# Feed-forward output of an encoder block: order of the loads, and the last normalisation on one engine

## The chip, the cores and the metric

The kernel runs on one core of one Trainium2 chip. The metric is device time in microseconds (us) of a whole execution, and versions are compared by the median of several runs. The engines are named as the profile names them: PE (TensorE) multiplies matrices, DVE (VectorE), ACT (ScalarE) and POOL (GpSimd) work on tiles element by element, SP (SyncE) here only issues DMA transfers. Each engine works through a queue of its own in order, and waits on semaphores for the others.

## The reference, cut to what matters

One layer of an encoder block on 1024 tokens of width 1024: a projection, dilated attention and a gated recurrence, then a feed-forward part (`D_FF` is 2816). The change lies in the last line, in the product with `w_ffn_out` and the layer norm behind it.

```python
def layer_norm(x, g, b):
    xf = x.astype(jnp.float32)
    mu = jnp.mean(xf, axis=-1, keepdims=True)
    xc = xf - mu
    var = jnp.mean(xc * xc, axis=-1, keepdims=True)
    y = xc * lax.rsqrt(var + LN_EPS) * g.astype(jnp.float32) + b.astype(jnp.float32)
    return y.astype(x.dtype)
...
    h = layer_norm(DEEPNORM_ALPHA * h + merged @ w_o[l], ln1_g[l], ln1_b[l])
    gate, up = jnp.split(h @ w_ffn_in[l], 2, axis=-1)
    h = layer_norm(DEEPNORM_ALPHA * h + (jax.nn.silu(gate) * up) @ w_ffn_out[l], ln2_g[l], ln2_b[l])
```

## The kernel before, in words

The whole kernel is one long program, built by a tile framework that tracks the dependencies of tiles, hands out buffers from pools (a tile waits until the last reader of the buffer's former tile is done) and orders each engine's instructions by a schedule of its own. Where the kernel fixes an order by hand, it does so with `ordered(key, ...)`: the loads of this stage are all made by `queued`, so they stay on SP in the order in which the program asks for them, and the splits and sums of this stage are `ordered` on DVE under the key `"sums"`.

Stage by stage there are the projection with attention and recurrence, the merge, `ffn_in` and at last `ffn_out`, which the change touches. `ffn_in` writes the gated activations and sums of them to DRAM, one tensor `gd[p]` for each of seven products.

`ffn_out` multiplies the activations (1024 tokens x 2816) with `w_ffn_out` (2816 x 1024) as a 2 x 2 block product with seven products instead of eight (Strassen's scheme in Winograd's form). Each product p has 512 tokens, 512 columns and a depth of 11 tiles of 128 (index f). The list `seq` holds the steps (p, f) of the products 1, 2, 6, 5, 3 and 7, 66 in all. The last product, 4, is done token block by token block in 12 `chunks` (three for each of the four blocks g of 128 tokens), so that its rows end one after another.

All values are float32. Each operand is split into a rounded part `hi` and a remainder `lo`, and `mm3` makes three matmuls: hi x hi, hi x lo, lo x hi. One step is 4 token blocks x 3 = 12 matmuls of 128x512. In the profile's names `gwsum` and `gwkeep` are hi and lo of the activations (three buffers each), `w_hi` and `w_lo` those of the weights (four). `hi` is cast by ACT (L212), `lo` is subtracted by DVE (L222). PE runs matmuls at L270, L271 and L272: L270 and L272 use `w_hi`, L271 uses `w_lo`.

`prep(i)` prepares step i, three steps ahead of the matmuls (`AHEAD = 3`). It calls `acts`, which takes care of the activation loads, then asks for weight tiles up to a count that grows with i, then splits the weights and makes the sums of weights that later products need (`extra`, L1767). Activations come in pairs (two f in one load of 512 KB, tile `a_raw`); three pairs are held, two in a pool with two buffers and one in another. Weights come in tiles of 256 KB: `11`, `21`, `12`, `22` are the blocks of the matrix, and the first six of block row 1 were loaded in whole rows (`w_rows`, L1683) by `ffn_in`. The loads of this stage are asked for in program order on SP, so a load that waits for its buffer holds back all loads behind it.

When a product is complete, `out` adds it from PSUM to the rows `Y[t]` (eight tiles of 128 tokens x 1024, L1791) and takes statistics (L1793). `finish(t)` makes the layer norm of a row tile: mean and variance (L206, L207), the power -1/2 by POOL (L208), and then one of two forms. Row tiles 6 and 7 take the mean out and multiply with g in one fused DVE operation (L1804), multiply with the power and add b in a second (L1807), each in two halves of 512 columns. Row tiles 0 to 5 take a longer way: a shift on DVE (L292), the normalisation on ACT (L293), the product with g on POOL (L1812), the sum with b on DVE (L1813). Rows 0 to 2 are finished in the middle of product 7 and early in the chunks; row 3 and rows 4 to 7 follow while the chunks run. `store` writes rows 0 to 5 to DRAM a few steps later, from SP (L1825).

Of the kernel before, what the change touches and what calls it, by code (L numbers as in the profile page):

```python
# [10 lines left out]
F32 = mybir.dt.float32  # L11
# [3 lines left out]
OP = mybir.AluOpType  # L15
# [7 lines left out]
HALF = 512  # L23
# [56 lines left out]
class Block:  # L80
# [1609 lines left out]
    def ffn_out(self):  # L1690
# [4 lines left out]
        nc, NP = self.nc, NF // 2  # L1695
        with ExitStack() as es:
            fob = es.enter_context(self.pool("fob"))
# [9 lines left out]
            Y = [fob.tile([128, D], F32, name=f"y{t}") for t in range(8)]  # L1707
            bn = [fob.tile([128, 2, 6], F32, name=f"st{t}") for t in range(8)]
            g2, b2 = (fob.tile([128, D], F32, name=n) for n in ("g2", "b2"))

            def load(z, f):
                i, k = int(z[0]) - 1, int(z[1]) - 1
                r = 128 * (2 * f + i)
                self.queued(W[z, f], self.wfo[r:r + 128, HALF * k:HALF * (k + 1)])

            seq = [(p, f) for p in (1, 2, 6, 5, 3, 7) for f in range(NP)]
            loads = [("11", f) for f in range(EARLY, NP)]
# [3 lines left out]
            pairs = [(p, f, n % 3) for n, (p, f) in enumerate(z for z in seq if z[1] % 2 == 0)]  # L1721
            loaded, raws, ready, last, t2s = 0, {}, {}, {}, {}
# [8 lines left out]

            def acts(p, f):

                while len(raws) < 3 and pairs:
                    q, k, m = pairs.pop(0)
                    n = min(2, NP - k)
                    raws[q, k] = (self.wraw, self.wraw, self.abp)[m].tile(
                        [128, 2, HALF], F32, name="a_raw", tag="wraw", bufs=(2, 2, 1)[m])
                    self.queued(raws[q, k][:, :n], self.gd[q][:, k:k + n])
                r = raws[p, f - f % 2]  # L1740
                if f % 2 or f + 1 == NP:
                    del raws[p, f - f % 2]
                return pair(r[:, f % 2])

            def pair(src):
                n = src.shape[1]
                hi, lo = (self.ws.tile([128, HALF], F32R, name=f"g{tag}", tag=tag, bufs=3)[:, :n]
                          for tag in ("wsum", "wkeep"))
                self.split(hi, lo, src, eng_lo="dve", key="sums")
                return hi, lo  # L1750

            def weights(src):
                hi, lo = (z.rearrange("p k c -> p (k c)") for z in self.granules())
                self.split(hi, lo, src, eng_lo="dve", key="sums")
                return hi, lo

            def extra(z, f):
                b = {k: W.get((k, f)) for k in ("11", "12", "21", "22")}
                if z == "last":
                    last[f] = place("11", f, F32R), place("12", f, F32R)  # L1760
                    self.split(*last[f], b["21"], eng_lo="dve", key="sums")
                    return
                if z == "t2":
                    t2s[f] = fob.tile([128, HALF], F32, name="t2", tag="t2", bufs=NP)
                out, x, y = {"t1": (b["11"], b["12"], b["11"]), "t2": (t2s.get(f), b["22"], b["11"]),
                             "t4": (b["21"], b["21"], t2s.get(f)), "t3": (b["12"], b["22"], b["12"])}[z]
                self.ordered("sums", nc.vector.tensor_sub(out, x, y))  # L1767

            def prep(i):
                nonlocal loaded  # L1770
                if i >= len(seq):
                    return
                p, f = seq[i]
                a = acts(p, f)
                while loaded < min(len(loads), 4 + 3 * i // 2):
                    load(*loads[loaded])
                    loaded += 1
                src = t2s[f] if p == 6 else W[{1: "11", 2: "21", 5: "11", 7: "12", 3: "22"}[p], f]
                ready[i] = a, weights(src)
                for z in todo.get(i, ()):  # L1780
                    extra(*z)
# [11 lines left out]
                    nc.vector.bn_stats(bn[g + 4 * i][:, k, :], y)  # L1793

            def finish(t):
                y, halves = Y[t], t > 5
                mv = self.tiny.tile([128, 4], F32, name="mv2", tag="bnmv", bufs=3)
                self.rstd(mv, bn[t])
                if halves:
                    for n in range(2):  # L1800
                        for k in range(2):
                            s = slice(HALF * k, HALF * (k + 1))
                            if n == 0:
                                nc.vector.scalar_tensor_tensor(y[:, s], y[:, s], mv[:, 0:1], g2[:, s],  # L1804
                                                               op0=OP.subtract, op1=OP.mult)
                            else:
                                nc.vector.scalar_tensor_tensor(y[:, s], y[:, s], mv[:, 2:3], b2[:, s],  # L1807
                                                               op0=OP.mult, op1=OP.add)
                                nc.sync.dma_start(self.out[128 * t:128 * (t + 1), s], y[:, s])
                else:  # L1810
                    self.normalise(fob, y, y, mv)
                    nc.gpsimd.tensor_mul(y, y, g2)  # L1812
                    nc.vector.tensor_add(y, y, b2)  # L1813

            stores = []

            def end(t, now):
                finish(t)
                if t < 6:
                    stores.append((now + 3, t))  # L1820
# [7 lines left out]
            for i in range(AHEAD):  # L1828
                prep(i)
            for i, (p, f) in enumerate(seq):  # L1830
                prep(i + AHEAD)
                store(i)
                (ahi, alo), (bhi, blo) = ready.pop(i)
                if p in (1, 6) and 4 <= f < 8:
                    t = f if p == 6 else f - 4
                    self.queued(Y[t], self.ahs_d[t])
                if p == 5 and f < 2:
                    t, v = (g2, b2)[f], self.ln["2"][f]
                    self.queued(t, bass.AP(tensor=v.tensor, offset=v.offset, ap=[[0, 128], [1, D]]))
                for g in range(4):  # L1840
                    if f == 0 and p == 2:
                        banks[g][1] = self.ps_sd()
                    c = slice(128 * g, 128 * (g + 1))
                    self.mm3(banks[g][p in (2, 5, 3)], ahi[:, c], alo[:, c], bhi, blo, p in (1, 2, 5) and f == 0,
                             f == NP - 1, skip_group_check=True)
                    if f == NP - 1:
                        out(p, g)
                if p == 7 and f in (4, 8):
                    end(f // 4 - 1, i)

            chunks = [(g, f) for g in range(4) for f in range(0, NP, 4)]
            halves, acts4 = {}, {}
# [70 lines left out]
```

## Time and profile before

| | |
|---|---|
| three runs | 2068.7, 2071.84, 2070.64 us, median 2070.64 |
| the profiled execution | 2068.59 us, of which the span from the first to the last instruction is 2066.8 |
| mean granted clock of PE | 0.994 |
| busy: PE, DVE, ACT, POOL | 2014.9, 1324.6, 953.3, 1078.9 us |
| product stage `ffn_out` | from about 1850 us to the end |

Times in the profile's rows are counted from the start of the span. A row of the timeline has start, duration, engine, line, operation, output and inputs, a count, and in brackets the idle time before it with what ended it. A row of waits has the waiting engine and line, the releaser, and total, count and longest. A row of a group has the count, then busy time and mean in ns, then idle time. A row of a stretch has from:to, its length, the busy time and count of PE, PE's weight loads, DVE, ACT and POOL, the granted clock, the DMA engines' busy share and GB/s. Operations of one engine overlap by about a tenth of a microsecond at their ends.

### The profile page before, as it was taken

What the parts mean: (1) busy time and instruction counts of PE and PEld (TensorE: products, weight loads), DVE (VectorE), ACT (ScalarE), POOL (GpSimd) and SP (SyncE); (2) the same over time, 40 slices, a digit from 0 to 9 for tenths busy, and PEclk for the clock granted to TensorE, in tenths of its full rate; (3) what the DMA queues carried; (4) which work ended last, traced back from release to release, by engine and by line L of the source; (5) the groups of instructions that cost most, each with busy time, mean ns of one, the idle gap of its engine ahead of it and who ended that gap; (6) DMA issues with size and microseconds to landing.
All of it is one profiled execution on the core that took longest, in us unless ns stands there. A gap on an engine that the chain in (4) does not pass through costs nothing. (4 is left out here: it accounts for less than half of the span.)

```text
span 2066.8 us, 30932 instructions
## 1 busy us (share of the span) xinstructions
PE 2014.9 (97%) x10974; PEld 1670.4 (81%) x10974; DVE 1324.6 (64%) x2017; ACT 953.3 (46%) x1968; POOL 1078.9 (52%) x919
## 2 busy tenths in 40 slices
PE   7899999999999999999999999999999999999998
PEld 5688888788888888888888888787888888878876
DVE  6867645884377844776343224657776776758777
ACT  6554455553555536555365432244433333344542
POOL 5767644686446653666536562344665665620012
PEclk9999999999999999999999999999999999999999
DMA  5434533335334352344524376444444343447423
GB/s 157 132 113 142 171 119 105 126 133 181 113 123 133 119 175 93 129 133 142 161 93 158 123 247 218 156 147 141 150 138 138 133 139 131 148 160 264 163 90 127
DMA packets 274845, 297.95 MB, mean 144 GB/s; under 512 B 14018, under 2 KB 207363, under 8 KB 274691
## 3 DMA queue, kind: packets, MB, share of 16 engines
q1 hardware_dynamic: 268384, 274.78, 41.3%
q10 hardware_dynamic: 6306, 21.20, 2.7%
q8 instruction: 86, 1.41, 0.3%
q14 instruction: 69, 0.56, 0.1%
HBM read 201.29 MB, written 94.63 MB: 143 GB/s over the span
## 5 line engine op out<-in xcount | busy, mean ns | idle before, releaser
L222 POOL TENSOR_TENSOR w_lo<-wa,w_hi 128x512 fp32r<-128x512 f32 x272 | 363.4, 1344 | 277.2 <-ACT w_hi L212 254.6
L212 ACT CAST w_hi<-wa 128x512 fp32r<-128x512 f32 x272 | 168.0, 619 | 251.1 <-PE pj L271 146.1
L222 POOL TENSOR_TENSOR w_lo<-wsum,w_hi 128x512 fp32r<-128x512 f32 x88 | 128.0, 1464 | 111.9 <-PE sd L272 60.7
L222 POOL TENSOR_TENSOR w_lo<-f_raw,w_hi 128x512 fp32r<-128x512 f32 x66 | 102.3, 1558 | 53.4 <-ACT w_hi L212 52.0
L208 POOL TENSOR_TENSOR mv<-mv,mhalf 128x1 f32<-128x1 f32 x16 | 10.7, 677 | 208.5 <-DVE mv L207 207.7
L212 ACT CAST w_hi<-wsum 128x512 fp32r<-128x512 f32 x88 | 54.7, 621 | 122.2 <-PE sd L271 118.7
L542 DVE TENSOR_TENSOR evh<-wkeep,pj 128x512 f32<-128x512 f32 x45 | 30.8, 685 | 111.9 <-PE pj L272 60.8
L270 PE MATMUL pj<-xt1hi,w_hi 128*128 128x512 f32 x252 | 99.7, 396 | 0.0
L270 PE MATMUL pj<-xb22hi,w_hi 128*128 128x512 f32 x252 | 99.2, 394 | 0.0
L272 PE MATMUL pj<-xb22hi,w_lo 128*128 128x512 f32 x252 | 98.3, 391 | 0.5 <-POOL w_lo L222 0.3
L271 PE MATMUL pj<-xb22lo,w_hi 128*128 128x512 f32 x252 | 98.6, 391 | 0.0
L272 PE MATMUL pj<-xt1hi,w_lo 128*128 128x512 f32 x252 | 98.6, 391 | 0.0
L271 PE MATMUL pj<-xt1lo,w_hi 128*128 128x512 f32 x252 | 98.6, 391 | 0.0
L212 ACT CAST gwsum<-a_raw 128x512 fp32r<-128x512 f32 (+1 forms) x78 | 47.7, 616 | 101.8 <-PE pj L271 42.5
L654 POOL TENSOR_TENSOR wa<-wa,wa 128x512 f32<-128x512 f32 x46 | 67.1, 1466 | 40.5 <-DVE wa L653 37.5
L222 DVE TENSOR_TENSOR gwkeep<-a_raw,gwsum 128x512 fp32r<-128x512 f32 (+1 forms) x78 | 57.8, 741 | 42.2 <-ACT gwsum L212 39.4
L222 POOL TENSOR_TENSOR w_lo<-ws,w_hi 128x512 fp32r<-128x512 f32 x46 | 62.4, 1358 | 43.0 <-ACT w_hi L212 42.4
L680 ACT COPY wkeep<-pj 128x512 f32<-128x512 f32 x136 | 79.1, 582 | 8.3 <-PE pj L272 5.7
L272 PE MATMUL pj<-xt2hi,w_lo 128*128 128x512 f32 x192 | 76.4, 398 | 4.6 <-POOL w_lo L222 4.6
L531 DVE TENSOR_TENSOR evh<-wkeep,pj 128x512 f32<-128x512 f32 x66 | 57.7, 878 | 34.8 <-PE pj L272 24.4
L270 PE MATMUL pj<-xt3hi,w_hi 128*128 128x512 f32 x192 | 77.0, 402 | 0.3 <-ACT wkeep L680 0.3
L270 PE MATMUL pj<-xt2hi,w_hi 128*128 128x512 f32 x192 | 76.4, 401 | 0.7 <-ACT w_hi L212 0.7
(421 smaller groups left out, 6586.3 us busy)
## 6 DMA issues: line engine op xcount, KB each, us to landing
wa<-in_w_in_dram SPq DMA_DIRECT2D x184, 256.0 KB, 3.3
f_raw<-in_w_ffn_in_dram SPq DMA_DIRECT2D x44, 512.0 KB, 4.1
a_raw<-gd SPq DMA_DIRECT2D x30, 512.0 KB, 3.7
gd<-fc SPq DMA_DIRECT2D x44, 256.0 KB, 2.0
gd<-fs SPq DMA_DIRECT2D x33, 256.0 KB, 2.1
tg<-evh SPq DMA_DIRECT2D x32, 256.0 KB, 2.3
tg<-tg SPq DMA_DIRECT2D x16, 512.0 KB, 4.1
y<-ahs SPq DMA_DIRECT2D x16, 512.0 KB, 4.8
```

What stands on the lines that cost most here:

```text
L208: nc.gpsimd.tensor_tensor(mv[:, 2:3], mv[:, 2:3], self.mhalf[:, 0:1], OP.pow)
L212: ins = nc.scalar.copy(hi, src) if eng_hi == "act" else nc.vector.tensor_copy(hi, src)
L222: ins = e.tensor_sub(lo, src, hi.bitcast(F32))
L270: nc.tensor.matmul(ps, whi, xhi, start=first, stop=False, **kw)
L271: nc.tensor.matmul(ps, whi, xlo, start=False, stop=False, **kw)
L272: self.product = nc.tensor.matmul(ps, wlo, xhi, start=False, stop=last, **kw).ins.name
L531: self.left(nc.vector.tensor_tensor(o, self.order_src(add, g, kind), s, OP.add))
L542: self.left(nc.vector.tensor_add(t, add, ps))
L654: nc.gpsimd.tensor_sub(a["a21"], a["a22"], a["a11"])
L680: nc.scalar.copy(t, ps)
```

## The change

Two edits, both in `ffn_out`.

1. In `acts`, the loop that asks for activation pairs is now a function `more`. It is called as before at the start, and once more right after the second half of a pair has been split, when the pair is dropped from the three that are held. So the next pair is asked for ahead of the weight tiles of that step, not behind them at the next step. The weight loads of step 0 (four tiles) are left to step 1 (`while i and ...`).
2. `finish` uses the two fused DVE operations for all eight row tiles. The shift, the normalisation on ACT and the product on POOL are gone. Rows 0 to 5 are still stored whole by `store`.

```diff
-                while len(raws) < 3 and pairs:
-                    q, k, m = pairs.pop(0)
...
+                def more():
+                    while len(raws) < 3 and pairs:
+                        q, k, m = pairs.pop(0)
...
+                more()
                 r = raws[p, f - f % 2]
+                out = pair(r[:, f % 2])
                 if f % 2 or f + 1 == NP:
                     del raws[p, f - f % 2]
-                return pair(r[:, f % 2])
+                    more()
+                return out
...
-                while loaded < min(len(loads), 4 + 3 * i // 2):
+                while i and loaded < min(len(loads), 4 + 3 * i // 2):
...
-                y, halves = Y[t], t > 5
+                y = Y[t]
...
-                if halves:
-                    for n in range(2):
-                        for k in range(2):
...
+                for n in range(2):
+                    for k in range(2):
+                        s = slice(HALF * k, HALF * (k + 1))
+                        if n == 0:
+                            nc.vector.scalar_tensor_tensor(y[:, s], y[:, s], mv[:, 0:1], g2[:, s],
+                                                           op0=OP.subtract, op1=OP.mult)
+                        else:
+                            nc.vector.scalar_tensor_tensor(y[:, s], y[:, s], mv[:, 2:3], b2[:, s],
+                                                           op0=OP.mult, op1=OP.add)
+                            if t > 5:
                                 nc.sync.dma_start(self.out[128 * t:128 * (t + 1), s], y[:, s])
-                else:
-                    self.normalise(fob, y, y, mv)
-                    nc.gpsimd.tensor_mul(y, y, g2)
-                    nc.vector.tensor_add(y, y, b2)
```

The new code shifts the lines below it: L1767, L1791, L1793, L1804, L1807 and L1825 are L1772, L1796, L1798, L1808, L1811 and L1826 in the changed kernel.

SP's queue at the end of `ffn_in`, as the difference of the two kernels. `gd_194` is the tensor of product 1's activations, `gd_197` and `gd_198` those of products 4 and 5:

```order
 L1625 DMA gd_194<-fc 128x512
 L1683 DMA w_rows<-in_w_ffn_out_dram 128x1024
+L249 DMA a_raw<-gd_194 128x1024
 L1625 DMA gd_197<-fc 128x512
 L1640 DMA gd_198<-fs 128x512
```

The fourth activation pair of product 1 is now asked for between the last whole weight row and the last six stores of `ffn_in`.

SP's queue a few rows on, in the first steps of `ffn_out`. `w_9` and `w_10` are the last tiles of block `11`, `w_0` to `w_3` tiles of blocks `21` and `22`:

```order
 L249 DMA w_9_17091<-in_w_ffn_out_dram 128x512
 L249 DMA w_10_17092<-in_w_ffn_out_dram 128x512
-L249 DMA a_raw<-gd_194 128x1024
 L249 DMA w_0_17093<-in_w_ffn_out_dram 128x512
 L249 DMA w_0_17109<-in_w_ffn_out_dram 128x512
+L249 DMA a_raw<-gd_194 128x1024
 L249 DMA w_1_17094<-in_w_ffn_out_dram 128x512
-L249 DMA a_raw<-gd_194 128x1024
 L249 DMA w_1_17110<-in_w_ffn_out_dram 128x512
 L249 DMA w_2_17095<-in_w_ffn_out_dram 128x512
+L249 DMA a_raw<-gd_194 128x512
```

The fourth pair has left this place, and each later pair stands one or two weight tiles further ahead.

DVE in product 7, before, from the power's argument of row 0 on (`y_17120` to `y_17122` are rows 0 to 2, `mv` their mean and power, `b_17137` is b):

```order
L207 TENSOR_SCALAR mv_18599<-mv_18599 128x1
L207 TENSOR_SCALAR mv_18692<-mv_18692 128x1
L222 TENSOR_TENSOR gwkeep<-a_raw,gwsum 128x512
L222 TENSOR_TENSOR w_lo<-w_rows,w_hi 128x512
L207 TENSOR_SCALAR mv_18783<-mv_18783 128x1
L292 SCALAR_TENSOR_TENSOR mv_18599<-mv_18599 128x1
L292 SCALAR_TENSOR_TENSOR mv_18692<-mv_18692 128x1
L222 TENSOR_TENSOR gwkeep<-a_raw,gwsum 128x512
L222 TENSOR_TENSOR w_lo<-w_rows,w_hi 128x512
L292 SCALAR_TENSOR_TENSOR mv_18783<-mv_18783 128x1
L1813 TENSOR_TENSOR y_17120<-y_17120,b_17137 128x1024
L222 TENSOR_TENSOR gwkeep<-a_raw,gwsum 128x512
```

The same place in the changed kernel, from the same row on (`g_17136` is g; x2 are the two halves):

```order
L207 TENSOR_SCALAR mv_18599<-mv_18599 128x1
L1808 SCALAR_TENSOR_TENSOR y_17120<-y_17120,mv_18599,g_17136 128x512 x2
L207 TENSOR_SCALAR mv_18692<-mv_18692 128x1
L1808 SCALAR_TENSOR_TENSOR y_17121<-y_17121,mv_18692,g_17136 128x512 x2
L222 TENSOR_TENSOR gwkeep<-a_raw,gwsum 128x512
L222 TENSOR_TENSOR w_lo<-w_rows,w_hi 128x512
L207 TENSOR_SCALAR mv_18783<-mv_18783 128x1
L1808 SCALAR_TENSOR_TENSOR y_17122<-y_17122,mv_18783,g_17136 128x512 x2
L1811 SCALAR_TENSOR_TENSOR y_17120<-y_17120,mv_18599,b_17137 128x512 x2
L222 TENSOR_TENSOR gwkeep<-a_raw,gwsum 128x512
L222 TENSOR_TENSOR w_lo<-w_rows,w_hi 128x512
L1811 SCALAR_TENSOR_TENSOR y_17121<-y_17121,mv_18692,b_17137 128x512 x2
```

The first `gwkeep` shown is that of step f = 4 of product 7, the second that of f = 5; four fused halves now stand ahead of each, two ahead of f = 6, and two with a weight sum ahead of f = 7.

DVE near the end, before, from the addition of row 6 (`y_17126`) to that of row 7 (`y_17127`):

```order
L1791 TENSOR_TENSOR y_17126<-y_17126,pj 128x512
L222 TENSOR_TENSOR gwkeep<-a_raw,gwsum 128x384
L1793 BN_STATS st_17134<-y_17126 128x6
L206 BN_AGGR mv_18942<-st_17134 128x2
L1813 TENSOR_TENSOR y_17125<-y_17125,b_17137 128x1024
L207 TENSOR_SCALAR mv_18942<-mv_18942 128x1
L1804 SCALAR_TENSOR_TENSOR y_17126<-y_17126,mv_18942,g_17136 128x512 x2
L1807 SCALAR_TENSOR_TENSOR y_17126<-y_17126,mv_18942,b_17137 128x512 x2
L1791 TENSOR_TENSOR y_17127<-y_17127,pj 128x512
```

The same place in the changed kernel, from the last fused operations of row 5 (`y_17125`) on:

```order
L1808 SCALAR_TENSOR_TENSOR y_17125<-y_17125,mv_18879,g_17136 128x512 x2
L1811 SCALAR_TENSOR_TENSOR y_17125<-y_17125,mv_18879,b_17137 128x512
L222 TENSOR_TENSOR gwkeep<-a_raw,gwsum 128x512
L1811 SCALAR_TENSOR_TENSOR y_17125<-y_17125,mv_18879,b_17137 128x512
L1796 TENSOR_TENSOR y_17126<-y_17126,pj 128x512
L222 TENSOR_TENSOR gwkeep<-a_raw,gwsum 128x384
L1798 BN_STATS st_17134<-y_17126 128x6
L206 BN_AGGR mv_18942<-st_17134 128x2
L207 TENSOR_SCALAR mv_18942<-mv_18942 128x1
L1808 SCALAR_TENSOR_TENSOR y_17126<-y_17126,mv_18942,g_17136 128x512 x2
L1811 SCALAR_TENSOR_TENSOR y_17126<-y_17126,mv_18942,b_17137 128x512 x2
L1796 TENSOR_TENSOR y_17127<-y_17127,pj 128x512
```

Row 5's last operation has moved from behind row 6's statistics to ahead of row 6's addition.

More of the change, by code (lines that the diff above doesn't have):

```diff
@@ L1732, in acts @@
             def acts(p, f):
-                while len(raws) < 3 and pairs:
-                    q, k, m = pairs.pop(0)
[L1736 to L1739, printed above, removed]
+                def more():
+                    while len(raws) < 3 and pairs:
+                        q, k, m = pairs.pop(0)
+                        n = min(2, NP - k)
+                        raws[q, k] = (self.wraw, self.wraw, self.abp)[m].tile(
+                            [128, 2, HALF], F32, name="a_raw", tag="wraw", bufs=(2, 2, 1)[m])
+                        self.queued(raws[q, k][:, :n], self.gd[q][:, k:k + n])
+                more()
                 r = raws[p, f - f % 2]
+                out = pair(r[:, f % 2])
                 if f % 2 or f + 1 == NP:
                     del raws[p, f - f % 2]
-                return pair(r[:, f % 2])
+                    more()
+                return out
             def pair(src):
@@ L1795, in finish @@
             def finish(t):
-                y, halves = Y[t], t > 5
+                y = Y[t]
                 mv = self.tiny.tile([128, 4], F32, name="mv2", tag="bnmv", bufs=3)
                 self.rstd(mv, bn[t])
-                if halves:
-                    for n in range(2):
-                        for k in range(2):
[L1802 to L1805, printed above, removed]
-                            else:
-                                nc.vector.scalar_tensor_tensor(y[:, s], y[:, s], mv[:, 2:3], b2[:, s],
-                                                               op0=OP.mult, op1=OP.add)
+                for n in range(2):
[8 more added lines that the diff above has]
+                            if t > 5:
                                 nc.sync.dma_start(self.out[128 * t:128 * (t + 1), s], y[:, s])
-                else:
-                    self.normalise(fob, y, y, mv)
-                    nc.gpsimd.tensor_mul(y, y, g2)
-                    nc.vector.tensor_add(y, y, b2)
             stores = []
```

## The prediction, made before the changed kernel was run

> **What bounds the kernel now.** First the head of the page, then the list of what TensorE (PE) waited for from 1690 us to the end, which holds the whole changed stage.
>
> ```profile
> span 2066.8 us, 30932 instructions
> PE 2014.9 (97%) x10974; PEld 1670.4 (81%) x10974; DVE 1324.6 (64%) x2017; ACT 953.3 (46%) x1968; POOL 1078.9 (52%) x919
> PE pj L271 <- DVE w_lo L222: 2.4, 1, 2.4
> PE pj L270 <- ACT gwsum L212: 1.5, 1, 1.5
> PE sd L270 <- DVE y L1791: 0.4, 1, 0.4
> ```
>
> PE is busy for 97% of the span, so a change in this stage can win only PE's few pauses and the piece after the last matmul. There are three pauses: A (1.5 us, for an activation tile), B (2.4 us, for DVE's weight remainder) and one of 0.4 us for an evacuation, which the change leaves. The timeline of PE gives the full loss of A and B. Each row is the first L271 of a step of 12 matmuls, except the second.
>
> ```profile
> 1855.56 0.39 PE L271 MATMUL pj<-w_lo,gwsum 128*128 128x512 f32 x1
> 1859.06 1.20 PE L270 MATMUL pj<-w_hi,gwsum 128*128 128x512 f32 x4 [1.53 <-ACT gwsum L212]
> 1863.25 0.39 PE L271 MATMUL pj<-w_lo,gwsum 128*128 128x512 f32 x1
> 2008.05 0.39 PE L271 MATMUL pj<-w_lo,gwsum 128*128 128x512 f32 x1
> 2020.51 0.39 PE L271 MATMUL pj<-w_lo,gwsum 128*128 128x512 f32 x1
> 2023.23 0.39 PE L271 MATMUL pj<-w_lo,gwsum 128*128 128x512 f32 x1
> ```
>
> An undisturbed step takes 2023.23 - 2020.51 = 2.72 us. From 1855.56 to 1863.25 are two steps: 7.69 - 5.44 = **2.25 us** lost at A. From 2008.05 to 2020.51 are three: 12.46 - 8.16 = **4.30 us** lost at B. B costs more than its wait because the granted clock is halved behind it, by the table of stretches (the third number from the end; 1.00 at most other places):
>
> ```profile
> 2015.00:2018.00 3.00, 3.00 (x9) 2.34 (x8) 3.00 (x6) 1.14 (x2) 0.00 (x0) 0.50 0.76 259
> ```
>
> By the Trainium skill (TensorE: Matmul & The Clock Gate, "What's actually happening") the clock halves after at least one idle window of about 3.4 us. By that rule the 2.40 us of B would leave the clock alone, B would be worth some 2.6 us, and the sum below 6.0. This trace disagrees: a wait of 2.40 us did halve it, and 4.30 is used.
>
> **Edit 1, the order of the loads.** Pause A, on ACT, SP and DVE:
>
> ```profile
> 1858.39 1.14 ACT L212 CAST gwsum<-a_raw 128x512 fp32r<-128x512 f32 x2 [2.92 <-DMA a_raw<-gd]
> 1861.75 1.19 ACT L212 CAST gwsum<-a_raw 128x512 fp32r<-128x512 f32 x2 [1.70 <-DMA a_raw<-gd]
> 1836.61 0.69 DVE L222 TENSOR_TENSOR gwkeep<-a_raw,gwsum 128x512 fp32r<-128x512 f32 x1
> 1832.84 0.33 SPq L1683 DMA_DIRECT2D w_rows<-in_w_ffn_out_dram  x1
> 1840.66 0.33 SPq L1625 DMA_DIRECT2D gd<-fc  x1
> 1851.38 0.43 SPq L249 DMA_DIRECT2D a_raw<-gd  x1
> 1858.00:1859.00 1.00, 0.00 (x0) 0.00 (x0) 0.00 (x0) 0.61 (x2) 0.00 (x0) 1.00 1.04 414
> ```
>
> ACT was late since the fourth activation pair (f = 6, 7 of product 1) landed at 1858.39, asked for at 1851.38 behind five weight tiles, while the DMA engines were full (share 1.04, 414 GB/s). In the new order this pair stands right behind the last `w_rows` load. Its buffer is that of the first pair, whose last reader is the DVE row at 1836.61 (to 1837.30). SP was idle from 1833.17 to 1840.66, so the load goes out at about 1837.3 and delays no `gd` store. With the 7.0 us of its old passage it lands at 1844.3, still 14 us early. The wait that this adds on SP costs nothing: behind it stand the six last `gd` stores, the first of which waited until 1840.66 anyway, and their readers are loads of much later products. Without that cover the stores would be late by what the pair waits, some 4 us from 1833.17 on, which only `gd` readers of products 2 to 7 could feel.
>
> What is late next is the fifth pair (f = 8, 9), landed at 1861.75. It loses the fourth pair (512 KB) and one weight tile (256 KB) ahead of it: 786 KB / 414 GB/s = 1.9 us, so some 1859.9. PE wants step 8 (its first L271) two steps behind step 6: 1855.56 + 3 x 2.72 = 1863.72, its first matmul 0.9 earlier. On ACT the cast of step 9's weights now stands ahead of this pair's; it waits for PE's end of step 5, before 1859.06, so not beyond the landing. Even a landing that stays at 1861.75 leaves 0.62 for the cast of one half before 1862.8. A weight that is now behind one more activation load moves back by 512 KB, 1.3 us, and all weights move forward by the same 1.3 us of the pair that is gone, so none lands later than now; PE needs them 2.25 us sooner, from a lead of three steps, 8.16 us. So A goes: **-2.25 us**; bounds 0 (another tile takes its place) and 2.25.
>
> **Edit 2, the last normalisation, at B.** DVE and POOL around B, then the groups of 1995 to 2067 us:
>
> ```profile
> 2004.05 8.08 POOL L1812 TENSOR_TENSOR y<-y,g 128x1024 f32<-128x1024 f32 x3 [1.66 <-ACT y L293]
> 2006.49 3.42 DVE L1813 TENSOR_TENSOR y<-y,b 128x1024 f32<-128x1024 f32 x1 [2.79 <-POOL y L1812]
> 2009.83 2.85 DVE L222 TENSOR_TENSOR gwkeep<-a_raw,gwsum 128x512 fp32r<-128x512 f32 x1
> 2013.20 1.21 DVE L1813 TENSOR_TENSOR y<-y,b 128x1024 f32<-128x1024 f32 x1
> ...
> L222 DVE TENSOR_TENSOR gwkeep<-a_raw,gwsum 128x512 fp32r<-128x512 f32 x17 | 14.4, 847 | 5.1 <-ACT gwsum L212 5.0
> L1813 DVE TENSOR_TENSOR y<-y,b 128x1024 f32<-128x1024 f32 x6 | 11.6, 1939 | 2.8 <-POOL y L1812 2.8
> L222 DVE TENSOR_TENSOR gwkeep<-a_raw,gwsum 128x384 fp32r<-128x384 f32 x4 | 4.1, 1025 | 0.5 <-ACT gwsum L212 0.5
> ```
>
> DVE first sat 2.79 us for POOL's product. Then, while POOL multiplied on to 2012.13, an addition that takes 1.21 alone took 3.42, and a remainder of 0.69 took 2.85, with the w_lo that PE waits for in line behind it. All three (idle, stretched addition, stretched remainder) go with POOL's multiplications. What comes instead:
>
> ```profile
> 1999.37 0.69 DVE L222 TENSOR_TENSOR w_lo<-w_rows,w_hi 128x512 fp32r<-128x512 f32 x1
> 1999.97 0.21 DVE L206 BATCH_NORM_AGGREGATE mv<-st 128x2 f32<-128x12 f32 x1
> 2000.09 0.17 DVE L207 TENSOR_SCALAR mv<-mv 128x1 f32<-128x1 f32 x2
> 2061.09 1.40 DVE L1804 SCALAR_TENSOR_TENSOR y<-y,mv,g 128x512 f32<-128x512 f32 x2
> 2062.41 1.41 DVE L1807 SCALAR_TENSOR_TENSOR y<-y,mv,b 128x512 f32<-128x512 f32 x2
> 2061.32 0.92 POOL L208 TENSOR_TENSOR mv<-mv,mhalf 128x1 f32<-128x1 f32 x1 [3.48 <-DVE mv L207]
> ```
>
> Two fused operations take 2062.41 - 2061.09 = 1.32 us, 0.66 each; a plain one 0.60 (1999.37 to 1999.97). Six rows of tiles need 24 fused: 15.8 us. What leaves DVE is 11.6 (additions) + 2.7 (17 remainders: 14.4 against 17 x 0.69) + 1.9 (four short ones: 4.1 against 4 x 0.55, the row at 2036.05 below): 16.2 us. So DVE is not loaded more, only in other places. In product 7 it goes, from 2000.16 on: the g pairs of rows 0 and 1 (4 x 0.66 + 0.07) and the two splits of step 4 (1.20) to 2004.07, wanted 2005.33; four fused and step 5 (3.91) to 2007.98, complete 0.09 later at 2008.07, wanted 2008.05; two fused and step 6 (2.52) to 2010.50, wanted 2010.77; two fused, one subtraction and step 7 (3.12) to 2013.62, complete 2013.71, wanted 2013.49; from then on 1.80 of work a step against 2.72. So PE still waits 0.2 to 0.3 us in all, and B gives **-4.0 us**. Bounds: 4.30 with no wait left; 3.0 if a fused operation takes its full 0.75 instead of 0.66 (12 x 0.09 = 1.1 more by step 7). ACT's lines L293 leave it, and its casts only come earlier. The output stores of rows 0 to 2 stand on SP between activation loads that wait for later remainders, so they hold nothing back.
>
> **Edit 2, at the end.**
>
> ```profile
> 2035.02 0.39 PE L272 MATMUL pj<-w,gwkeep 128*128 128x512 f32 x1
> 2035.44 0.69 DVE L1791 TENSOR_TENSOR y<-y,pj 128x512 f32<-128x512 f32 x1 [0.92 <-PE pj L272]
> 2036.05 0.55 DVE L222 TENSOR_TENSOR gwkeep<-a_raw,gwsum 128x384 fp32r<-128x384 f32 x1
> ...
> 2051.16 0.68 DVE L1791 TENSOR_TENSOR y<-y,pj 128x512 f32<-128x512 f32 x1
> 2057.46 0.39 PE L272 MATMUL pj<-w,gwkeep 128*128 128x512 f32 x1
> 2059.33 0.68 DVE L1791 TENSOR_TENSOR y<-y,pj 128x512 f32<-128x512 f32 x1
> ```
>
> A waiting DVE adds 0.42 us after the last matmul starts (2035.02 to 2035.44). For the last row that would be 2057.88, but DVE was still on row 6 and came at 2059.33. In the new order row 5 is done before row 6's addition. Even if that stays at 2051.16, row 6 needs 1.76 from its addition to its first fused operation (row 7: 2059.33 to 2061.09), a short remainder of 0.55 in between and 2.64 fused: DVE is free at 2056.1, 1.8 us ahead of 2057.88. Everything behind the last addition stays: **-1.45 us**, at worst 0.
>
> **Sum.** -2.25 - 4.0 - 1.45 = -7.7 us. The profiled execution took 2068.59 us (span 2066.8 and 1.8 around it): 2060.9 for its like. The median of the three runs is 2070.64, 2.05 above it: **2062.9 us**. By 0.2% (4.1 us) a measurement of this kernel can tell two versions apart.
>
> **Rivals.**
>
> *POOL's small powers hold DVE.* By the Trainium skill (SBUF - State Buffer, "Who interferes with whom") a DVE instruction with two SBUF inputs contends with a POOL instruction that reads SBUF, and the loser blocks for the whole of the other. As a mechanism here: the three powers of rows 0 to 2 hold DVE at the worst place, step 5.
>
> ```profile
> 2000.29 2.10 POOL L208 TENSOR_TENSOR mv<-mv,mhalf 128x1 f32<-128x1 f32 x3 [167.47 <-DVE mv L207]
> ```
>
> Were DVE held for all 2.10, w_lo of step 5 would come 2.1 late; B is left with 4.30 - 2.4 = 1.9, or 0.2 when the clock halves again (1.7). Sum 3.9 to 5.6: 2065.0 to 2066.7. Against it: the two fused operations from 2061.09 ran at their normal 1.40 beside a power of 0.92. Chance 0.12.
>
> *A weight tile takes pause A's place*, in product 1 or 2. For it: the DMA engines are full there (414 GB/s), PE comes 2.25 us sooner, and activations now go ahead of weights. Then A is lost and 4.0 + 1.45 remain: 2065.2. Against it: no weight lands later than now, and today PE waits for none. Chance 0.12.
>
> *SP's queue blocks (slower).* Each pair is now asked for as soon as its buffer's last reader is queued, and weights stand behind it.
>
> ```profile
> SPq L249 <- DVE gwkeep L222: 12.1, 5, 3.8
> ```
>
> The place is SP in products 1 and 2. It decides once a hold of weights exceeds the preparation's lead of three steps, 8.16 us. If six pairs each hold them by a step, 16.3 - 8.2 = 8.1 us of PE waits, with three halved clocks 5.1 more, less the 5.45 of the rest: +7.8, 2078.4. Against it: SP's longest wait for DVE is 3.8 us (the last number of the row), less than half of the lead, and the pairs it waits for are released by the step that DVE has done three steps ahead of PE. Chance 0.06.
>
> **Chances.** The forecast has 0.70. Faster by over 0.2%: 0.69 of it, 0.11 of the weight rival, 0.06 of the power rival, 0.86; slower 0.06; the same 0.08. The range goes from 2062.6 (all three at their best, 8.0) less the 1.6 by which runs of one kernel differ (half of 2068.7 to 2071.84), 2061.0, up to the worst power rival, 2066.7, with a little added: 2060.7 to 2067.0.
>
> **What would show it.** Right: no wait of PE for gwsum near 1858, none over 0.5 us for w_lo near 2008 to 2013 and no 0.50 clock there, no DVE row above 0.8 us for 128x512 after 2000, and the last addition 0.42 after the last matmul. Wrong: a new PE wait for w_lo or gwsum of over 1 us between 1855 and 1900, or fused rows of 0.8 us and more in product 7.

## The result, and the profile after

The new kernel takes **2062.56 us** (median of 6 runs, 2061.19 to 2064.15) against 2069.14 (6 runs, 2068.16 to 2071.84) for the kernel before: ratio 0.9968, 95% interval 0.9958 to 0.9978, that is 6.6 us less (4.6 to 8.7). Timed again in a second session (the last experiment), the ratio was 0.9964 [0.9951, 0.9978]. The forecast was 2062.9 us, and faster.

The profiled execution of the new kernel took 2064.15 us, with a span of 2062.3. First the head of its page:

```profile
span 2062.3 us, 30940 instructions
...
PE 2015.5 (98%) x10974; PEld 1670.5 (81%) x10974; DVE 1326.1 (64%) x2029; ACT 947.6 (46%) x1962; POOL 1063.9 (52%) x913
```

Then all that TensorE waited for from 1690 us to the end (us in total, times, longest):

```profile
PE sd L270 <- DVE y L1796: 0.4, 1, 0.4
```

Of the three pauses only the evacuation's 0.4 us is left; A (for `gwsum`) and B (for `w_lo`) are gone. DVE is about as busy as before (1326.1 against 1324.6 us); the forecast had 0.4 us less. The fused operations cost what POOL's interference and the plain additions had cost.

The two profiled spans differ by only 4.5 us, though, because the profiled execution of the new kernel reached the changed stage 2.85 us later. Upstream both kernels are the same program; a halved granted clock is likely to be part of this, since the clock records show seven halved windows of 3.41 us ahead of the stage in this profile and five in that of before (see the last section). So the changed stage is compared by itself: from the start of the last matmul `sd<-xt4hi,w_lo` of the product before to the start of the last pair of fused operations of row 7 (`y<-y,mv,b`). In the profile before this is 1846.72 to 2062.41, 215.69 us; in the profile after, 1849.57 to 2057.66, **208.09 us**. The change is worth 7.60 us there; the sum of the prediction was 7.7.

SP's queue and the casts of ACT at the place of pause A, after (start, duration, engine, line, operation):

```profile
1835.68 0.33 SPq L1683 DMA_DIRECT2D w_rows<-in_w_ffn_out_dram  x1
1840.17 0.33 SPq L249 DMA_DIRECT2D a_raw<-gd  x1
1843.50 0.33 SPq L1625 DMA_DIRECT2D gd<-fc  x1
...
1861.92 0.62 ACT L212 CAST gwsum<-a_raw 128x512 fp32r<-128x512 f32 x1 [0.83 <-DMA a_raw<-gd]
```

The fourth pair is asked for at 1840.17 (1837.3 in the prediction's clock, plus 2.85), and the first `gd` store behind it goes out at 1843.50, which is 1840.66 + 2.84: SP's wait held nothing back. Only the fifth pair is still waited for by ACT, and TensorE does not feel it.

POOL in product 7, after, and then DVE, both by the timeline:

```profile
2000.88 0.98 POOL L208 TENSOR_TENSOR mv<-mv,mhalf 128x1 f32<-128x1 f32 x1 [165.23 <-DVE mv L207]
2002.26 0.99 POOL L208 TENSOR_TENSOR mv<-mv,mhalf 128x1 f32<-128x1 f32 x1 [0.40 <-DVE mv L207]
2004.85 0.99 POOL L208 TENSOR_TENSOR mv<-mv,mhalf 128x1 f32<-128x1 f32 x1 [1.60 <-DVE mv L207]
```

```profile
2004.68 1.41 DVE L1808 SCALAR_TENSOR_TENSOR y<-y,mv,g 128x512 f32<-128x512 f32 x2
2006.01 1.41 DVE L1811 SCALAR_TENSOR_TENSOR y<-y,mv,b 128x512 f32<-128x512 f32 x2
...
2007.93 0.69 DVE L222 TENSOR_TENSOR w_lo<-w_rows,w_hi 128x512 fp32r<-128x512 f32 x1
...
2010.46 0.70 DVE L222 TENSOR_TENSOR w_lo<-w,w_hi 128x512 fp32r<-128x512 f32 x1
...
2013.59 0.70 DVE L222 TENSOR_TENSOR w_lo<-w,w_hi 128x512 fp32r<-128x512 f32 x1
```

No DVE row is stretched. The remainders of steps 5, 6 and 7 end at 2008.62, 2011.16 and 2014.29. The prediction's ends, 2008.07, 2010.59 (2010.50 and the 0.09 until it is complete) and 2013.71, are in the clock of the profile before; with 2.85 for the later start and less the 2.25 of pause A they are 2008.67, 2011.19 and 2014.31. The pairs of 1.41 stand right beside POOL's powers (that of 2004.68 beside 2004.85 to 2005.84) and are as long as in the tail.

In the table of stretches, the granted clock (third number from the end) where it had been 0.50 is now full:

```profile
2015.00:2018.00 3.00, 3.00 (x15) 2.48 (x14) 2.97 (x6) 0.62 (x1) 0.00 (x0) 1.00 0.29 83
```

By the timeline the last addition of row 7 comes 0.43 us behind the start of the last matmul (2054.14), in place of 1.87. The second row is the last pair, whose start ends the measured stage:

```profile
2054.57 0.69 DVE L1796 TENSOR_TENSOR y<-y,pj 128x512 f32<-128x512 f32 x1 [2.50 <-PE pj L272]
...
2057.66 1.41 DVE L1811 SCALAR_TENSOR_TENSOR y<-y,mv,b 128x512 f32<-128x512 f32 x2
```

### The profile page after: what moved, and what is told of

It reads as the page before. It is cut to its first block, busy times and chain, and to the rows that moved or that the text cites. A ratio compares the mean times of both kernels' runs of the same rounds, so it can differ in the third digit from the quotient of the medians.

```text
span 2062.3 us, 30940 instructions
## 1 busy us (share of the span) xinstructions
PE 2015.5 (98%) x10974; PEld 1670.5 (81%) x10974; DVE 1326.1 (64%) x2029; ACT 947.6 (46%) x1962; POOL 1063.9 (52%) x913
## 3 DMA queue, kind: packets, MB, share of 16 engines
q8 instruction: 86, 1.41, 0.3%
## 5 line engine op out<-in xcount | busy, mean ns | idle before, releaser
L270 PE MATMUL pj<-xt4hi,w_hi 128*128 128x512 f32 x192 | 76.1, 396 | 0.8 <-ACT w_hi L212 0.8
L270 PE MATMUL pj<-xb11hi,w_hi 128*128 128x512 f32 x192 | 76.9, 402 | 0.0
```

The costliest lines, as they stand in the source:

```text
L270: nc.tensor.matmul(ps, whi, xhi, start=first, stop=False, **kw)
```

## The experiments

Each experiment was read by the same stage, since run times of one kernel spread over 3 to 13 us, and experiments 5 to 8 ran once each. The first four were timed in one session, against 25 runs of the kernel before (2070.84 median, 2063.95 to 2076.52).

**1. The order of the loads alone.** The new `acts` and `prep`, with the old `finish`; against the new kernel:

```
-    y = Y[t]
+    y, halves = Y[t], t > 5
...
+    else:
+        self.normalise(fob, y, y, mv)
+        nc.gpsimd.tensor_mul(y, y, g2)
+        nc.vector.tensor_add(y, y, b2)
```

> Edit 1 alone: the loads are asked for in the new order, the last normalisation is that of before. The measure is the stage from the start of the last matmul of ffn_in (output sd, input xt4hi, w_lo) to the start of the last pair of fused operations of row 7: 215.69 us before, 208.09 us with both edits. My theory (three separate terms): pause A goes, pause B and the late last addition stay: stage 213.4 us (-2.25), PE waits 2.4 us for w_lo in product 7 and the clock halves behind it, no wait for gwsum near 1858. Time ratio to the kernel before 0.9989. Rival (edit 2 brings all, A would be made up for later because B's wait absorbs whatever PE gains): stage 215.7, ratio 1.000.

Measured: stage 213.44 us, 2.25 less than before; ratio 0.9987 [0.9973, 1.0000]. TensorE's waits in the stage are B and the evacuation, no longer A:

```profile
PE pj L271 <- DVE w_lo L222: 2.4, 1, 2.4
PE sd L270 <- DVE y L1796: 0.4, 1, 0.4
```

So edit 1 is worth pause A, and no other tile took its place. The stage of this one profile shows it; the run times alone do not, since their interval reaches 1.0000.

**2. The fused normalisation alone.** The old order of the loads, the new `finish`; against the new kernel:

```
-    def more():
-        while len(raws) < 3 and pairs:
+    while len(raws) < 3 and pairs:
...
-        more()
...
-    while i and loaded < min(len(loads), 4 + 3 * i // 2):
+    while loaded < min(len(loads), 4 + 3 * i // 2):
```

> Edit 2 alone: the two fused operations for all rows, the loads in the order of before. My theory: A stays with its 1.5 us wait for gwsum (2.25 us lost), B and the late last addition go: stage 210.3 us (-5.4), ratio 0.9974. Rival (edit 2 brings all): stage 208.1, ratio 0.9963, and A's wait is seen but costs nothing at the end. Rival (the terms depend on each other, since without A's gain the loads run 2.25 us ahead of PE): anything else than the difference of the other two runs, by more than 0.3 us.

Measured: stage 210.26 us, 5.43 less; ratio 0.9969 [0.9958, 0.9980]. A stays, B is gone, and the last addition lags by 0.43:

```profile
PE pj L270 <- ACT gwsum L212: 1.4, 1, 1.4
PE sd L270 <- DVE y L1791: 0.4, 1, 0.4
```

The two halves add up: 2.25 + 5.43 = 7.68 against 7.60 for both.

**3 and 4. The fused normalisation for some rows only**: for rows 0 to 2, which are finished in product 7, or for rows 3 to 5, which are finished in product 4. The edit is one condition in the `finish` of the kernel before (the stores by halves stay with rows 6 and 7).

```
-    y, halves = Y[t], t > 5
+    y, halves = Y[t], t > 5 or t < 3      # 3
+    y, halves = Y[t], t > 2               # 4
```

> Edit 2 for rows 0 to 2 alone, in product 7; rows 3 to 5 keep ACT, POOL and DVE, the loads are those of before. My theory: B goes with its halved clock (4.0 us, with 0.2 to 0.3 us of PE waits left by my count, 0 by the profile with both edits), the last addition stays 1.9 us behind the last matmul: stage 211.5 us (-4.2), ratio 0.9980. Rival (the gain at B is only the 2.4 us wait, and the halved clock comes anyway at another place of the stage): stage 213.3.

Measured: stage 211.87 us, 3.82 less (expected 211.5), the last addition still late by 1.89; ratio 0.9970 [0.9960, 0.9980]. That ratio would be 6.2 us, more than the stage shows; where the rest of it comes from, the one profile does not tell.

> Edit 2 for rows 3 to 5 alone, while the chunks of product 4 run; rows 0 to 2 keep ACT, POOL and DVE, the loads are those of before. My theory: A and B stay, the last addition starts 0.43 us behind the last matmul instead of 1.87: stage 214.25 us (-1.44), ratio 0.9993. B's wait is again 2.4 us and the clock halves again. Rival (the late last addition was an after-effect of B, DVE never caught up): the last addition stays 1.9 us late, stage 215.7.

Measured: stage 212.55 us, 3.14 less, where 1.45 was expected (214.25); ratio 0.9986 [0.9976, 0.9996]. The last addition lags by 0.43, as it should: rows 3 to 5 are the term at the end, rows 0 to 2 are B. But 1.7 us more went than expected. The stage has the same 899 matmuls in every profile, and the start of the n-th, set against that of the n-th in the new kernel, tells where time is lost. At A it is 1.72 us here and 2.25 in the first profile of before, since TensorE's wait there was smaller (first fence, 1.0 against 1.5). At B it is 2.74 us here and 3.91 there. So 0.53 of the 1.7 us is the smaller A, and 1.17 is B. Yet TensorE's wait at B is there in full, as the row that ends it shows (second fence); what is missing is the halved clock behind it (third fence):

```profile
PE pj L270 <- ACT gwsum L212: 1.0, 1, 1.0
```

```profile
2013.30 0.50 PE L271 MATMUL pj<-w_lo,gwsum 128*128 128x512 f32 x1 [2.39 <-DVE w_lo L222]
```

```profile
2013.50:2016.50 3.00, 3.00 (x13) 2.23 (x13) 3.00 (x5) 1.14 (x2) 0.00 (x0) 1.00 0.43 162
2016.50:2019.50 3.00, 3.00 (x13) 2.21 (x13) 2.97 (x5) 0.62 (x1) 0.00 (x0) 1.00 0.77 274
```

In experiment 1 the same wait was followed by half the clock:

```profile
2005.81 0.50 PE L271 MATMUL pj<-w_lo,gwsum 128*128 128x512 f32 x1 [2.40 <-DVE w_lo L222]
```

```profile
2006.50:2009.00 2.50, 2.50 (x8) 1.91 (x7) 2.50 (x5) 0.23 (x1) 0.00 (x0) 0.50 0.52 195
```

A pause of 2.4 us thus sometimes halves the clock and sometimes doesn't. That is worth 1.17 us here, and not the 1.7 us by which 3.41 us at half the clock are longer for a TensorE that is always busy: at the full clock TensorE ran into DVE's next remainders, which were still late. The first `w_lo` matmuls of its next two steps follow at 2.94 and 2.95 us (from the 2013.30 above) in place of 2.72:

```profile
2016.24 0.50 PE L271 MATMUL pj<-w_lo,gwsum 128*128 128x512 f32 x1
2019.19 0.50 PE L271 MATMUL pj<-w_lo,gwsum 128*128 128x512 f32 x1
```

Experiment 8 takes up the clock.

**5. POOL's multiplications by themselves.** Three products that nobody reads, behind the power of row 2; every engine keeps the order of all else, so nothing waits for their result.

```
-    self.rstd(mv, bn[t])
+    power = self.rstd(mv, bn[t])
+    for n in range(3 if t == 2 else 0):
+        self.behind(nc.gpsimd.tensor_mul(spare, g2, b2), power.ins.name)
```

> The new kernel, with three multiplications of 128x1024 added on POOL behind the power of row 2, on a tile that nobody reads; the order of every other instruction on every engine stays. They need 8.1 us, from about 4 us after the power of row 0. Theory (POOL's multiplications stretch DVE's operations with two inputs; in the kernel before 1.9 us of DVE work took 6.3 beside them): in 8.1 us DVE does 2.5 us of its work and loses 5.6, of which 0.3 to 1 is slack: TensorE waits some 5 us for w_lo in one or two pieces, and the stage (start of the last matmul sd<-xt4hi,w_lo to the start of the last fused pair) takes 213.1 us, 214.8 with one halved window of the clock behind it, in place of 208.1. Rival (what cost time before was DVE's queue standing still for POOL's product, not the memory): no DVE row stretched, no wait, 208.1.

Measured: stage 217.03 us, 8.94 more than the new kernel. POOL, DVE and TensorE there by the timeline, and then the table of stretches:

```profile
2005.77 8.04 POOL L1806 TENSOR_TENSOR spare<-g,b 128x1024 f32<-128x1024 f32 x3
2005.97 5.64 DVE L1814 SCALAR_TENSOR_TENSOR y<-y,mv,b 128x512 f32<-128x512 f32 x2
2011.53 2.83 DVE L222 TENSOR_TENSOR gwkeep<-a_raw,gwsum 128x512 fp32r<-128x512 f32 x1
2014.28 0.68 DVE L222 TENSOR_TENSOR w_lo<-w_rows,w_hi 128x512 fp32r<-128x512 f32 x1
2015.01 0.79 PE L271 MATMUL pj<-w_lo,gwsum 128*128 128x512 f32 x1 [6.25 <-DVE w_lo L222]
```

```profile
2015.50:2018.50 3.00, 3.00 (x8) 2.32 (x8) 3.00 (x6) 0.10 (x1) 0.00 (x0) 0.50 0.68 257
2018.50:2021.00 2.50, 2.50 (x7) 1.92 (x6) 2.46 (x5) 1.04 (x2) 0.00 (x0) 0.50 0.55 206
```

POOL's three operations take 8.04 us (2.68 each), and beside them DVE gets just three through: the pair that takes 1.41 elsewhere took 5.64, the remainder of 0.69 took 2.83. DVE gets one operation through for each of POOL's. Nothing waits for these three results, so it is the running beside each other that costs, and not a wait in DVE's queue. That is the theory in kind, but its price was too low: TensorE waited 6.25 us in one piece, not 5, and the clock stayed halved for three windows, in which the work from 2015.0 to 2021.0 took twice its time. By the Trainium skill (SBUF - State Buffer, "Who interferes with whom") the loser of this contention blocks for the whole of the other's instruction; this run's 5.64 and 2.83 agree. For POOL's small powers, the rival of the prediction, the rows after showed no such hold.

**6. The fourth pair put back.** The new kernel without the condition at step 0, by which only the fourth pair moves on SP.

```
-    while i and loaded < min(len(loads), 4 + 3 * i // 2):
+    while loaded < min(len(loads), 4 + 3 * i // 2):
```

> The new kernel, with the loads of weights allowed at step 0 again: on SP only the fourth activation pair moves, from ahead of the last gd stores to between the weights w11_9 and w11_10, one place earlier than in the kernel before; the other pairs stay early. Theory (pause A was this one pair's landing): one weight of 256 KB at 414 GB/s less ahead of it, 0.6 us earlier than before, so TensorE still waits some 0.9 us for gwsum there, and the stage takes 209.6 us (208.1 + 1.5). Rival (the early order of all pairs is what counts): no wait, 208.1. Other rival (the gd stores ahead of the loads are the cause): the whole of A is back, 210.3.

Measured: stage 209.15 us, 1.06 more than the new kernel (1.5 expected). By the timeline, ACT's casts behind the late landing, and then TensorE:

```profile
1862.67 1.14 ACT L212 CAST gwsum<-a_raw 128x512 fp32r<-128x512 f32 x2 [1.69 <-DMA a_raw<-gd]
1863.34 1.19 PE L270 MATMUL pj<-w_hi,gwsum 128*128 128x512 f32 x4 [0.30 <-ACT gwsum L212]
```

A pause is back with this one pair, and the early order of the others does not take it away. It costs more than its listed wait of 0.30 us (0.9 expected), as A did in the profile before (1.53 listed, 2.25 lost). That all 2.25 us of edit 1 hang on this pair is not shown, since 1.06 came back. How much one place in the queue is worth stays open as well: the wait at A was 0.30 us here, but in five profiles with the old order it ran from 0.7 to 1.6 by itself, so 0.6 us cannot be read out of one run.

**7. Without POOL, but not fused.** ACT normalises rows 0 to 5, DVE multiplies and adds over 128x1024.

```
+    if t < 6:
+        self.normalise(fob, y, y, mv)
+        nc.vector.tensor_mul(y, y, g2)
+        nc.vector.tensor_add(y, y, b2)
+        return
```

> The new kernel, with rows 0 to 5 normalised in three steps again: ACT normalises, and DVE, not POOL, multiplies by g and adds b, 128x1024 each at 1.21 us (1.13 from start to start). Theory (POOL's multiplications were the cost, and the fusing saves little): DVE is no more loaded than by four fused operations (2.3 against 2.6 us a row); ahead of step 6 of product 7 stand five such operations from about 4 us after the power of row 0, and its w_lo comes within 0.3 us of when TensorE wants it: the stage takes 208.1 to 208.4 us. Rival (without the fusing, the chain ACT, DVE, DVE is late): a wait for w_lo of over 1 us, 209.5 or more.

Measured: stage 208.30 us, 0.21 more than the new kernel, and no wait of TensorE in the list (which has those over 0.15 us) but the evacuation's. DVE's longest queue there, with the remainder behind it:

```profile
2000.84 2.36 DVE L1806 TENSOR_TENSOR y<-y,g 128x1024 f32<-128x1024 f32 x2 [0.30 <-ACT y L293]
2003.12 1.22 DVE L1807 TENSOR_TENSOR y<-y,b 128x1024 f32<-128x1024 f32 x1
2004.26 1.22 DVE L1806 TENSOR_TENSOR y<-y,g 128x1024 f32<-128x1024 f32 x1
2005.39 1.22 DVE L1807 TENSOR_TENSOR y<-y,b 128x1024 f32<-128x1024 f32 x1
...
2007.13 0.69 DVE L222 TENSOR_TENSOR w_lo<-w,w_hi 128x512 fp32r<-128x512 f32 x1
```

Five operations of 1.22 pass before the remainder, and it is late by some 0.26 us: it ends at 2007.82, and the first `w_lo` matmul of TensorE's step follows 2.98 us after that of the step before, in place of 2.72. That is about what this version loses.

```profile
2004.89 0.39 PE L271 MATMUL pj<-w_lo,gwsum 128*128 128x512 f32 x1
2007.87 0.50 PE L271 MATMUL pj<-w_lo,gwsum 128*128 128x512 f32 x1
```

What the edit needs is that POOL stays out; whether DVE fuses hardly counts.

**8. The kernel before, once more.**

> The kernel before, unchanged, profiled once more. Theory on the clock (it is decided on a fixed grid of windows of 3.41 us, which lies elsewhere in each run, and a window in which TensorE stands still for over some 1.95 us is followed by one at half the clock): the waits of 1.5 and 2.4 us are there again; that of 2.4 us is followed by a halved clock if over 1.95 us of it lie in one window (for 56% of all places of the grid), and the stage takes 215.7 us then and 214.0 otherwise; the one of 1.5 us never is. Rival (a wait of 2.4 us always halves the clock): 215.7 in every run.

Measured: stage 214.75 us (1848.98 to 2063.73). The end of B by the timeline, half the clock behind it by the table of stretches, and A by the list of waits, smaller than in the first profile:

```profile
2014.77 0.79 PE L271 MATMUL pj<-w_lo,gwsum 128*128 128x512 f32 x1 [2.41 <-DVE w_lo L222]
```

```profile
2014.50:2017.50 3.00, 2.73 (x7) 2.15 (x7) 3.00 (x5) 0.00 (x0) 0.00 (x0) 0.50 0.27 108
```

```profile
PE pj L270 <- ACT gwsum L212: 0.7, 1, 0.7
```

Of the wait, 63% of one window of the clock's grid was filled, so the theory wanted the halved clock; the run agrees, but the rival ("always") wants it too and falls by experiment 4 alone. Neither had the 0.94 us less, nearly all of it A's (1.42 us lost in place of 2.25): with the same instructions in the same order, the wait at A was 0.7 us here and 1.5 there.

**9 and 10. The unfused version and the new kernel, timed side by side** in a second session, against 17 runs of the kernel before (2069.40 median).

> The kernel of the DVE-unfused experiment again, now timed in rounds against the kernel before: if only the stage counts (208.3 us there, against 208.1 in the new kernel and 215 in the kernel before), it is as much faster than the kernel before as the new one, 6 to 7 us, ratio 0.9968, and the two cannot be told apart. Rival (its ACT work or its order of TensorE's last product costs time that one profile did not show): ratio above 0.9978.

> The new kernel again, unchanged, timed in rounds on the chip of the run beside it, so that the two can be compared: ratio to the kernel before 0.9965 (stage 208.1 against 215.2 on the mean of the two profiles of before, 7.1 us of 2069), and no pause of TensorE over 0.4 us in the stage.

Measured: the new kernel 2062.12 us, 0.9964 [0.9951, 0.9978], stage 208.11; the unfused one 2065.26 us, 0.9976 [0.9964, 0.9988], stage 208.33. The intervals overlap, and 0.9976 with its interval decides nothing between the expected 0.9968 and a rival that starts at 0.9978. Both profiles have the evacuation's 0.4 us as their only listed wait in the stage. If the unfused version is slower by more than its 0.2 us, these runs do not show it; none tried beats the new kernel.

## Why the prediction was right

- **Edit 1, 2.25 us**: shown by experiment 1, to the hundredth, by one profile of each kernel. The step that was missing is that A is no fixed size: the wait was 1.53 us in the first profile of before, 1.4, 1.6, 1.0 and 0.7 in the others with the old order of loads, since it is the race between a landing and TensorE's arrival.
- **Edit 2 at B, 4.0 us**: the mechanism is shown by experiments 3 (rows 0 to 2 alone give 3.82), 5 (POOL's multiplications alone bring a larger pause back) and 7 (without them, unfused, no stop of TensorE over 0.3 us). TensorE's part of the stage fell by 6.17 us in all, from 210.74 to 204.57, where A and B were put at 6.25. The working of DVE's queue held to 0.05 us.
- **Edit 2 at the end, 1.45 us**: the lag of the last addition went from 1.87 to 0.43. Experiment 4 shows that rows 3 to 5 alone do it.
- **What was mis-sized** is the halved clock inside B, counted as certain and at 1.7 us since the one profile showed it. In the three profiles with B and a halved clock behind it (both of before, experiment 1) B lost 3.91, 3.80 and 3.91 us; without it, in experiment 4, 2.74, so it is worth 1.1 to 1.2 us. It was also argued from that one trace that a wait of 2.40 us halves the clock. The Trainium skill (TensorE: Matmul & The Clock Gate, "What's actually happening") has the clock halve after at least one idle window of about 3.4 us. The runs agree with neither: it depends on where the wait falls, by the last section. An estimate from its 44 of 100 executions without a halved clock takes about 0.5 us from B in the mean. A lost 2.25, 2.16, 2.33, 1.72 and 1.42 us in the five profiles with the old order of loads, 2.0 in the mean. With both, the mean gain is nearer to 7 than to 7.7 (3.4 + 2.0 + 1.45); the two ratios give 6.6 and 7.4.
- **The rivals**: the powers of 0.98 and 0.99 us held nobody (rows of 1.41 beside them); no weight tile took A's place (experiment 1); SP's queue blocked nothing (the `gd` store at 1843.50).

That the median came within 0.4 us of the forecast is partly chance: the base of 2070.64 was 1.2 to 1.5 us above two of the three larger samples of the kernel before (2069.40 and 2069.14; the third has 2070.84), and the gain was put about as much too high.

## What to carry to other kernels

Beside wide GpSimd operations DVE got one two-input operation through for each of GpSimd's here; look for DVE rows that are several times as long as their like, and count the work that stands behind them rather than the idle time ahead. In a queue of loads look for the one transfer that is late: moving its neighbours alone did not take the pause away (experiment 6). What one profile shows behind a short pause of TensorE (a halved clock, the size of a race) is one draw of several, so compare the changed stage in more than one profile before putting that down as a fixed price. And the price of a halved clock is smaller where another engine would have made TensorE wait anyway.

## What the hardware showed beyond that

The clock's changes lie on a grid. In the records of the granted clock in twelve profiles (two of the new kernel, two of the kernel before, the rest from the experiments) every halved stretch between 100 and 2040 us is 3.41 us long or two or three times that, and the changes of one run are whole multiples of 3.41 us apart; where the grid lies differs from run to run. With TensorE's pauses of over 0.15 us laid over that grid, each window in which it stood still for at least 40% of the time was decided by the share: from 0.574 up (27 windows) the clock was halved behind it, up to 0.566 (24 windows) it was not. That is some 1.95 us of one window. The waits at B fit: shares of 0.608, 0.632 and 0.704 halved the clock, the 0.479 of experiment 4 did not, and the waits of 1.4 to 1.6 us at A never did (0.41 to 0.46). A wait of 2.4 us lies so that neither of two neighbouring windows gets 1.95 us for (2 x 1.95 - 2.4) / 3.41 = 44% of the grid's places: an estimate from these numbers, not counted in runs.

Two things don't fit and stay open. At one place upstream, a wait of 1.97 us near 1436 us, the clock was halved in five profiles behind a window with a share of only 0.27 to 0.36, and in a sixth it was not at 0.27; and a window already at half the clock was followed by a further one at shares of 0.16 to 0.25. The threshold is thus read from these pauses, and what the gate counts is not shown.

The same pauses upstream, at about 390, 905, 1332 and 1436 us, are in both kernels, and each can halve the clock or not, for up to 1.7 us (half of 3.41, an estimate; at B it was 1.17). The profiled execution of the new kernel had all four halved, its second profile three, and one of experiment 1 none; they reached the changed stage at 1849.57, 1845.77 and 1841.45 us. This is likely to be one reason why executions of one kernel differ by several us. It is not the only one: both profiles of the kernel before have five halved windows ahead of the stage and reach it 2.26 us apart (1846.72 and 1848.98).
